# Counting the SBUF way that VectorE and GpSimd share, and TensorE's rates, in a kernel's own list scheduler

## The chip, the cores and the metric

The kernel runs on one core of a Trainium2 chip. The metric is the device time of one launch in microseconds. The engines are named as in the profile: PE is TensorE (PEld its weight loads), DVE is VectorE, ACT is ScalarE, POOL is GpSimd, SP is SyncE, whose queue here only starts DMAs. SBUF is the on-chip memory that all engines read, PSUM the banks into which PE writes.

## The reference, cut to what matters

Two layers of a decoder trunk over 512 tokens of width 1024, all in float32. Each layer has one input projection, three kinds of attention side by side (native sparse attention with compressed, selected and window parts; stick-breaking; forgetting attention), an output projection, a cross attention over 256 memory tokens, and a gated MLP with a causal convolution of three taps.

```python
for i in range(DEPTH):                                   # 2
    h = rms_norm(x, norm_mix[i])
    (q_n, kc, vc, ks_, vs_, kw, vw, g_n,
     q_s, k_s, v_s, q_f, k_f, v_f, f_l) = split_columns(h @ w_in[i])
    ...
    o = jnp.concatenate([o_nsa, o_sb, o_fox], axis=2).reshape(B, S, MIX_WIDTH).astype(x.dtype)
    x = x + o @ w_out[i]
    m = rms_norm(mem, norm_mem[i])
    x = x + memory_cross_attention(rms_norm(x, norm_cross[i]), m,
                                   w_mq[i], w_mk[i], w_mv[i], w_mo[i])
    x = x + conv_gated_mlp(rms_norm(x, norm_ffn[i]), w_up[i], conv_w[i], conv_b[i], w_down[i])
return rms_norm(x, norm_final)

def conv_gated_mlp(h, w_up, conv_w, conv_b, w_down):
    u = h @ w_up                                         # 1024 -> 5632
    u = lax.conv_general_dilated(u, ...) + conv_b        # 3 taps over the tokens
    gate, val = u[..., :D_FF], u[..., D_FF:]
    return (jax.nn.silu(gate) * val) @ w_down
```

## The kernel before, in words

**Numbers in two parts.** A float32 operand of a large product is kept as a high part (rounded to the type fp32r) and a low part (what the rounding left), and a product is three matmuls: high by high, high by low, low by high (`proj_k`). So each weight tile that a DMA brings (`wr`, a "raw" buffer; there are 6) goes through `split`: a cast makes the high part (`w`, ACT or DVE may do it), and a subtraction the low part (also named `w`, DVE or POOL may do it). The pair of `w` tiles is what PE reads; there are 8 such tiles, and the raw buffer is free for the next DMA only after the subtraction.

**Activations.** The residual stream stands in 8 tiles `x` (128 features by 512 tokens). `Norm.tile` makes for each tile the scaled high part `hh` (ACT or DVE), the low part `hl` (DVE alone, a scalar_tensor_tensor), and the square `sq` (ACT), which is added to the running sum `sa` (DVE or POOL). `rstd_bcast` splits `sa` into `ah` and `al`, sums over partitions on PE (`acc`), and ACT makes the reciprocal root `rstd`.

**Stages.** The start loads the `x` tiles and the first weights, and runs the first projections (`pj` tiles in PSUM) together with the norm of the memory tokens (`mem_norm`: tiles `msq`, `mem`, `mh`, `ml`, 16 stores to DRAM named `mk`) and the compression of keys and values (`comp` and `job_comp`: tile `kcx`, whose products start a short chain that ends in the compressed keys `kc`). Then come the attention items of the layer with projections as filler. The cross stage starts with the last part of the output projection (`add_product` with `wout_c`, by halves of the tokens, each tile followed by `nrm2.tile`), goes through the cross attention (`cross_map`), and ends with its output projection (`add_product` with `wmo`, followed by `nrm3.tile`). Then comes the MLP: 22 pairs of up-projections (24 matmuls each), whose results go through `u` and `cv` on DVE and ACT to `gh` and `gl`, and 16 down-projections of 33 matmuls each.

**What sets the order.** All instructions are first recorded as `Op`s, each with its engine (or several that may do it, `alts`), a cost in ns, and dependencies taken from the regions that it reads and writes. `Plan.run` then goes through a planned time: for each engine `pick` takes the first recorded instruction that is ready and whose buffers can be had; `better` passes it over where another allowed engine would end it earlier by the planner's clocks; and the engine with the earliest start goes next. What comes out is the order of each engine's instructions, and for instructions with `alts` the engine. The chip then runs every engine's list strictly in that order, with semaphores between engines. The planner's costs are no times of the chip: they only decide order and place. `Engine.__getattr__` gives each matmul its cost, `_cost` gives the others theirs: of a tensor_tensor over 512 elements 1225 ns on POOL, and 595 on DVE plus the penalty `PEN` of 245 ns that `better` adds for DVE.

The lines of before that the change touches are these:

```python
end = max(t, op.ready[e]) + op.alts[e][1] + self.PEN[e]        # better
...
c = max(64, n) / 2.4                                           # matmul of n columns
if args[1].buf.dtype == FT:
    part = args[1].p1 - args[1].p0 <= 64 or out.p1 - out.p0 <= 64
    c = max(c * (2 if part else 4), 107 if part else 214)
...
return self.plan.add("PE", name, outs, ins, fn, max(c, 104) + 3)
```

In the profile nearly every instruction has the line of the helper that calls it in the end (L385), so groups are told apart by the names of their tiles.

Of the kernel before, what the change touches and what calls it, by code (L numbers as in the profile page):

```python
# [140 lines left out]
class Op:  # L141
    __slots__ = ("i", "eng", "fn", "cost", "tail", "deps", "after", "wait", "ready", "new", "bufs", "prio", "end", "name", "alts")


class Plan:


# [26 lines left out]
    def add(self, eng, name, outs, ins, fn, cost, tail=0, alts=()):  # L174
        op = Op()
        op.alts = {eng: (fn, cost)}
        op.alts.update(alts)
        op.i, op.eng, op.fn, op.cost, op.tail, op.name = len(self.ops), eng, fn, cost, tail, name
        op.prio = op.i + self.bias
        op.deps, op.after, op.new, op.bufs, op.end = {}, [], [], [], None  # L180
        for views, wr in ((ins, False), (outs, True)):
            for v in views:
                b = v.buf
# [23 lines left out]
    def run(self):  # L207
# [16 lines left out]
        for op in self.ops:  # L224
            if not op.wait:
                for e in op.alts:
                    heapq.heappush(soon[e], (0.0, op.prio, op.i))
        dma = 0.0
        order = []
# [33 lines left out]
        def better(e, op, t):  # L263

            if len(op.alts) == 1:
                return False
            end = max(t, op.ready[e]) + op.alts[e][1] + self.PEN[e]
            for x, (_, c) in op.alts.items():
                if x != e and max(clock[x], op.ready[x]) + c + self.PEN[x] < end:
                    c += sum(ops[i].alts[x][1] for p, i in avail[x] if p < op.prio and not done[i])  # L270
                    if max(clock[x], op.ready[x]) + c + self.PEN[x] < end:
                        return True
            return False

        def pick(e):
            t = clock[e]
            while soon[e] and soon[e][0][0] <= t:
                r, p, i = heapq.heappop(soon[e])
                if not done[i]:
                    heapq.heappush(avail[e], (p, i))  # L280
            tried, got, no = [], None, set()
            while avail[e]:
                x = heapq.heappop(avail[e])
                if done[x[1]]:
                    continue
                tried.append(x)
                op = ops[x[1]]
                kinds = {b.kind for b in op.bufs if not b.held}
                if kinds & no:
                    continue  # L290
                if room(op):
                    if better(e, op, t):
                        continue
                    got = op
                    break
                no |= kinds
            for x in tried:
                heapq.heappush(avail[e], x)
            if got is not None:
                return max([t, got.ready[e]] + [min(free[b.kind]) for b in got.bufs if b.kind is not None and not b.held]), got  # L300
            for r, p, i in sorted(soon[e]):
                if not done[i] and room(ops[i]) and not better(e, ops[i], t):
                    return max([t, r] + [min(free[b.kind]) for b in ops[i].bufs if b.kind is not None and not b.held]), ops[i]
            return None

        cand = {e: None for e in self.engines}
        while len(order) < len(ops):
# [10 lines left out]
            for b in made[op.i]:  # L318
# [5 lines left out]
                live[k].append(b)  # L324
            clock[e] = start + op.cost
            op.end = start + op.cost
            if op.tail:
# [25 lines left out]
class Engine:  # L353
# [17 lines left out]
    def __getattr__(self, name):  # L371
        def call(out, *args, **kw):
# [26 lines left out]
            if name == "matmul":  # L399
                n = args[1].size()  # L400
                c = max(64, n) / 2.4
                if args[1].buf.dtype == FT:
                    part = args[1].p1 - args[1].p0 <= 64 or out.p1 - out.p0 <= 64
                    c = max(c * (2 if part else 4), 107 if part else 214)
                if not kw.get("start"):
                    ins = ins + [out]
                return self.plan.add("PE", name, outs, ins, fn, max(c, 104) + 3)
            if name == "transpose":
# [1312 lines left out]
```

## Time and profile before

| | us |
|---|---|
| median of 3 timed runs | 1514.27 |
| lowest and highest of them | 1512.98, 1520.28 |
| the profiled execution, its own time | 1519.45 |
| its span from first to last instruction | 1517.7 |
| PE busy, of that span | 1450.1 |
| DVE, ACT, POOL busy | 1109.1, 669.4, 402.0 |

Busy time is the share in which at least one instruction of an engine is under way. PE's matmuls overlap (a matmul of 512 columns is shown with some 390 ns, but the next starts after 233), so a busy PE is not a PE at its peak. An instruction of DVE or POOL that has started and cannot go on is shown as busy, with a longer duration. The clock granted to TensorE is given as a share of full speed; it is 0.5 or 1 at any moment. A row of the timeline may stand for several instructions of one form (x2, x3): its time is then from the first start to the last end, and the time in square brackets is the idle time before it, with what ended it.

### The profile page before, as it was taken

How to read it: one execution, taken by the hardware profiler on the slowest of the kernel's cores; microseconds unless marked ns; L12 is line 12 of the kernel's file. 1: busy time of each engine (PE TensorE's matmuls, PEld its weight loads, DVE VectorE, ACT ScalarE, POOL GpSimd, SP SyncE). 2: the span in 40 equal slices, each digit the busy share in tenths (PEclk: the TensorE clock that was granted, in tenths of full speed). 3: DMA queues.
4: the chain of work that ended last, by engine and by line, in shares of the span. 5: the costliest groups of instructions: out<-in, count | busy, mean ns of one | idle time of the engine just before them, and what ended most of it. 6: DMA issues, size and time to landing. Idle time of an engine off the chain costs nothing.

```text
span 1517.7 us, 21473 instructions
## 1 busy us (share of the span) xinstructions
PE 1450.1 (96%) x7478; PEld 1156.8 (76%) x7478; DVE 1109.1 (73%) x2166; ACT 669.4 (44%) x1490; POOL 402.0 (26%) x337
## 2 busy tenths in 40 slices
PE   7899999988899999999999999999789999999997
PEld 5777677777888788888887766877778887888886
DVE  7876857789978835887575686677989785378864
ACT  5356566747533213223333656674574322123321
POOL 5321112352422212221143111124542221122111
PEclk9899999999999999999999999999999999999998
DMA  8620214034123233322433121412312223323232
GB/s 260 220 77 29 63 43 129 32 105 132 56 98 97 70 104 105 97 95 83 157 116 99 38 63 49 125 47 83 109 44 91 82 82 92 111 91 97 76 100 69
DMA packets 88556, 140.99 MB, mean 93 GB/s; under 512 B 13088, under 2 KB 35904, under 8 KB 88448
## 3 DMA queue, kind: packets, MB, share of 16 engines
q1 hardware_dynamic: 85696, 136.65, 28.9%
q0 software_dynamic: 1120, 1.41, 0.4%
q10 hardware_dynamic: 1632, 1.57, 0.3%
q8 instruction: 58, 0.95, 0.3%
q14 instruction: 50, 0.41, 0.1%
HBM read 125.04 MB, written 8.39 MB: 88 GB/s over the span
## 4 chain that ended last, share of the span: by engine, by line
PE 72%; DVE 20%; issue 3%; ACT 3%; DMA 2%; SPq 0%; DVEq 0%; ACTq 0%
PE pj L385 39%; PE S L385 25%; DVE w L385 4%; PE acc L385 4%; PE T L385 3%; DVE cv L385 3%; DVE hl L385 2%; DVE x L385 2%; ACT cv L385 1%; DMA wr<-in_dram 1%; DVE u L385 1%; DVE sa L385 1%; DVE sp L385 1%; ACT cp L385 0%; SPq L385 0%
## 5 line engine op out<-in xcount | busy, mean ns | idle before, releaser
L385 POOL TENSOR_TENSOR w<-wr,w 128x512 fp32r<-128x512 f32 (+4 forms) x212 | 299.7, 1420 | 817.1 <-PE pj L385 378.9
L385 PE MATMUL pj<-hh,w 128*128 128x512 f32 (+1 forms) x1376 | 436.7, 389 | 11.6 <-ACT hh L385 7.9
L385 PEld LDWEIGHTS pj<-hh,w 128*128 128x128 f32 x1376 | 256.6, 192 | 68.5 <-ACT hh L385 9.0
L385 ACT ACTIVATE w<-wr 128x512 fp32r<-128x512 f32 (+4 forms) x288 | 160.9, 584 | 284.5 <-PE pj L385 175.7
L385 DVE TENSOR_TENSOR w<-wr,w 128x512 fp32r<-128x512 f32 (+4 forms) x256 | 207.9, 826 | 103.4 <-PE S L385 45.1
L385 PE MATMUL pj<-hl,w 128*128 128x512 f32 (+1 forms) x688 | 265.6, 386 | 2.4 <-DVE hl L385 2.3
L385 PE MATMUL S<-hh,w 128*128 128x512 f32 (+1 forms) x736 | 230.1, 385 | 0.0
L385 DVE SCALAR_TENSOR_TENSOR cv<-u,conv,cv 128x510 f32<-128x510 f32 (+1 forms) x176 | 153.2, 873 | 69.2 <-ACT cv L385 66.0
L385 PEld LDWEIGHTS S<-hh,w 128*128 128x128 f32 x736 | 136.8, 188 | 29.9
L385 PEld LDWEIGHTS pj<-hl,w 128*128 128x128 f32 x688 | 132.0, 192 | 29.8 <-DVE hl L385 5.8
L385 DVE CAST w<-wr 128x512 fp32r<-128x512 f32 (+4 forms) x180 | 77.0, 443 | 94.5 <-PE pj L385 40.4
L385 ACT ACTIVATE cv<-u,conv 128x512 f32<-128x512 f32 x88 | 71.5, 815 | 163.1 <-DVE u L385 163.1
L385 PE MATMUL S<-hl,w 128*128 128x512 f32 (+1 forms) x368 | 141.6, 385 | 0.0
L385 PE MATMUL pj<-oh,w 128*128 128x512 f32 (+1 forms) x320 | 102.6, 373 | 13.8 <-DVE x L385 13.2
L385 PE MATMUL S<-gh,w 128*128 128x512 f32 (+1 forms) x396 | 114.8, 369 | 0.0
L385 PE MATMUL pj<-gh,w 128*128 128x512 f32 x352 | 113.4, 395 | 0.2
L385 ACT ACTIVATE P<-P,nmx 128x512 f32<-128x512 f32 (+3 forms) x160 | 87.9, 552 | 28.9 <-DVE nmx L385 28.6
L385 DVE CUSTOM_DVE_ANT_0 P<-S,maskq 128x512 f32<-128x512 f32 (+3 forms) x160 | 70.4, 486 | 31.7 <-PE S L385 29.7
L385 PEld LDWEIGHTS pj<-oh,w 128*128 128x128 f32 x320 | 60.2, 190 | 28.6 <-DVE x L385 15.4
L385 PEld LDWEIGHTS S<-gh,w 128*128 128x128 f32 x396 | 71.6, 188 | 13.6
L385 PE MATMUL pj<-w,hh 128*128 128x280 f32 (+2 forms) x384 | 80.9, 305 | 0.0
L385 PEld LDWEIGHTS S<-hl,w 128*128 128x128 f32 x368 | 69.2, 188 | 14.9
(266 smaller groups left out, 2460.8 us busy)
## 6 DMA issues: line engine op xcount, KB each, us to landing
wr<-in_dram SPq DMA_DIRECT2D x292, 256.0 KB
wr<-in_dram SPq DMA_DIRECT2D x112, 192.0 KB
wr<-in_dram SPq DMA_DIRECT2D x48, 128.0 KB
x<-in_dram SPq DMA_DIRECT2D x16, 256.0 KB
wr<-in_dram SPq DMA_DIRECT2D x8, 280.0 KB
wr<-in_dram SPq DMA_DIRECT2D x8, 260.0 KB
cw<-in_dram SPq DMA_DIRECT2D x8, 256.0 KB
mk<-mh SPq DMA_DIRECT2D x8, 256.0 KB
```

The lines of the kernel that those rows point to most:

```text
L385: return getattr(eng, name)(real(out), *[real(a) for a in args], **{k: real(v) for k, v in kw.items()})
```

## The change

Two things change in the planner, and nothing in what is computed. First, each `Op` gets a flag `port`, set when none of its tiles is in PSUM and it is no DMA. The planner keeps one time `port` for VectorE and GpSimd together: an instruction with the flag, on either of the two, can't start in the plan before the last one with the flag has ended, on either of the two. `better` counts that wait when it compares engines, and `pick` prefers an instruction that need not wait for it. Second, a matmul's cost is 0.455 ns for each column (at least 110 ns), so that 512 columns cost 233 ns where 216.3 stood; the float32 forms follow 0.835 ns a column, twice that where rows and columns are all in use.

```diff
@@ Plan.add
+        op.port = not tail and not any(v.buf.bank for v in list(ins) + list(outs))
@@ Plan.run
-        dma = 0.0
+        dma = port = 0.0
@@ better
-            end = max(t, op.ready[e]) + op.alts[e][1] + self.PEN[e]
+            end = max(t, op.ready[e], held(op, e)) + op.alts[e][1] + self.PEN[e]
             for x, (_, c) in op.alts.items():
-                if x != e and max(clock[x], op.ready[x]) + c + self.PEN[x] < end:
+                if x != e and max(clock[x], op.ready[x], held(op, x)) + c + self.PEN[x] < end:
                     c += sum(ops[i].alts[x][1] for p, i in avail[x] if p < op.prio and not done[i])
-                    if max(clock[x], op.ready[x]) + c + self.PEN[x] < end:
+                    if max(clock[x], op.ready[x], held(op, x)) + c + self.PEN[x] < end:
                         return True
             return False
+        def held(op, e):
+            return port if op.port and e in ("DVE", "POOL") else 0.0
@@ pick
                     if better(e, op, t):
                         continue
+                    if held(op, e) > t:
+                        later = later or op
+                        continue
                     got = op
                     break
...
+            got = got or later
             if got is not None:
-                return max([t, got.ready[e]] + [...]), got
+                return max([t, held(got, e), got.ready[e]] + [...]), got
@@ Plan.run, after an instruction is placed
             clock[e] = start + op.cost
+            if op.port and e in ("DVE", "POOL"):
+                port = clock[e]
@@ Engine, matmul
-                c = max(64, n) / 2.4
+                c = max(0.455 * n, 110)
                 if args[1].buf.dtype == FT:
                     part = args[1].p1 - args[1].p0 <= 64 or out.p1 - out.p0 <= 64
-                    c = max(c * (2 if part else 4), 107 if part else 214)
+                    c = max(0.835 * n, 107) * (1 if part else 2)
...
-                return self.plan.add("PE", name, outs, ins, fn, max(c, 104) + 3)
+                return self.plan.add("PE", name, outs, ins, fn, c)
```

Both programs hold the same instructions; order and place differ. POOL's list goes from 342 instructions with operands to 226, DVE's from 2168 to 2182, ACT's from 1306 to 1413. The largest moves by kind: of the subtractions for `w` of 512 columns 149 stood on POOL and 93 do now; of the casts for `w` of 512 columns 109 stood on DVE and 38 do now (the others are on ACT); of the additions to `sa` by halves 35 stood on POOL and 8 do now.

In the rows that follow, a name is the program's tile with its number, an underscore and a running number of the build, and the last column is the shape written.

The start of POOL's list, before, behind its constants: `w18` to `w24` are the low parts of the first weights, `sa66` is the sum of squares, `w147` and `w163` the low parts of the next weights, `mem` the memory tokens.

```order
L385 TENSOR_TENSOR w18_148<-wr29_130,w17_144 128x256
L385 TENSOR_TENSOR sa66_146<-sa66_146,sq67_166 128x512
L385 TENSOR_TENSOR w20_196<-wr38_142,w19_185 128x256
L385 TENSOR_TENSOR w20_196<-wr43_162,w19_185 128x256
L385 TENSOR_TENSOR sa66_146<-sa66_146,sq69_211 128x512
L385 TENSOR_TENSOR w22_246<-wr48_182,w21_234 128x256
L385 TENSOR_TENSOR w22_246<-wr53_206,w21_234 128x256
L385 TENSOR_TENSOR sa66_146<-sa66_146,sq71_260 128x512
L385 TENSOR_TENSOR w24_293<-wr58_230,w23_282 128x256
L385 TENSOR_TENSOR w24_293<-wr63_258,w23_282 128x256
```

The same place of POOL's list in the changed program:

```order
L399 TENSOR_TENSOR msq94_402<-msq94_402,msq98_424 128x512
L399 TENSOR_TENSOR w147_456<-wr148_365,w146_437 128x560
L399 DMA rot15_77<-u87_447 8x512 x2
L399 DMA rot16_78<-u125_454 8x512 x2
L399 DMA kcx89_574<-in_18_dram 128x8x2
L399 TENSOR_TENSOR t1124_460<-t1124_460,rot16_78 128x512
L399 TENSOR_TENSOR t1134_515<-t1134_515,rot15_77 128x512
```

All of the first weights' low parts and sums of squares have moved to DVE, and POOL's first instruction with operands is one of the memory norm.

PE's list at the reciprocal root of the memory tokens, before: `acc101` sums the squares over partitions and waits for DVE's `ah` and `al`; `pj133` is the second projection, `pj154` the first tile of a third one of 280 columns.

```order
L385 MATMUL pj133_419<-hh61_299,w23_282 128x512
L385 MATMUL acc101_483<-ah102_469,ones12_74 128x256
L385 MATMUL pj133_419<-hl62_313,w23_282 128x512
L385 MATMUL acc101_483<-al103_480,ones12_74 128x256
L385 MATMUL acc101_483<-ah104_476,ones12_74 128x256
L385 MATMUL pj133_419<-hh61_299,w24_293 128x512
L385 MATMUL acc101_483<-al105_485,ones12_74 128x256
L385 MATMUL pj154_497<-w146_455,hh26_140 128x280
```

And in the changed program:

```order
L399 MATMUL pj158_489<-w146_437,hh26_140 128x280
L399 MATMUL pj158_489<-w147_456,hh26_140 128x280
L399 MATMUL pj154_474<-w147_456,hh36_177 128x280
L399 MATMUL acc101_497<-ah102_487,ones12_74 128x256
L399 MATMUL pj154_474<-w146_437,hl37_187 128x280
L399 MATMUL pj154_474<-w146_437,hh41_203 128x280
L399 MATMUL pj154_474<-w147_456,hh41_203 128x280
L399 MATMUL acc101_497<-al103_495,ones12_74 128x256
L399 MATMUL acc101_497<-ah104_491,ones12_74 128x256
```

`acc101` stands behind all of `pj133` and in the midst of `pj154` now. The first product of `kcx` (`pj126`) has moved behind 13 more matmuls of 280 columns; the second (`pj136`) stands at nearly the same place, and the same 264 matmuls stand ahead of the first `S` in both lists. On SP the loads of the weight for `pj187` (`wr185`, `wr186`) stood ahead of the 16 stores `mk`, and stand behind 15 of them now; on DVE one subtraction for `w151`, the low part that the second half of `pj154` reads, stood ahead of `kcx` and stands behind all of `ml` now.

DVE's list at the beginning of the cross stage, before: `x` takes a product tile (`pj` or `S`, both in PSUM), `hh` and `hl` are its two parts.

```order
L385 TENSOR_TENSOR x727_797<-x727_797,pj878_3505 128x256
L385 TENSOR_SCALAR hh875_3536<-x699_453,gains3_65 128x256
L385 SCALAR_TENSOR_TENSOR hl872_3543<-x688_432,gains3_65,hh871_3524 128x256
L385 SCALAR_TENSOR_TENSOR hl876_3552<-x699_453,gains3_65,hh875_3536 128x256
L385 TENSOR_TENSOR x752_804<-x752_804,S882_3511 128x256
L385 SCALAR_TENSOR_TENSOR hl880_3566<-x727_797,gains3_65,hh879_3549 128x256
L385 TENSOR_TENSOR x760_2357<-x760_2357,pj886_3516 128x256
L385 TENSOR_TENSOR x785_2361<-x785_2361,S890_3521 128x256
L385 SCALAR_TENSOR_TENSOR hl884_3585<-x752_804,gains3_65,hh883_3572 128x256
```

And in the changed program, from the same row:

```order
L399 TENSOR_TENSOR x727_596<-x727_596,pj878_3502 128x256
L399 TENSOR_SCALAR hh875_3528<-x699_426,gains3_65 128x256
L399 SCALAR_TENSOR_TENSOR hl872_3535<-x688_408,gains3_65,hh871_3516 128x256
L399 SCALAR_TENSOR_TENSOR hl876_3543<-x699_426,gains3_65,hh875_3528 128x256
L399 TENSOR_TENSOR sa873_3525<-sa873_3525,sq877_3533 128x256
L399 SCALAR_TENSOR_TENSOR hl880_3557<-x727_596,gains3_65,hh879_3541 128x256
L399 TENSOR_TENSOR sa873_3525<-sa873_3525,sq881_3549 128x256
L399 TENSOR_TENSOR x752_751<-x752_751,S882_3508 128x256
```

The additions to `sa`, which POOL did beside these rows, stand among them on DVE. Over one cross stage (from the first `x` to the last `hl` of `nrm3`) 15 additions to `sa` and 6 subtractions for `w` of 512 columns go from POOL to DVE, 2 and 3 of them the other way; 13 rows go from DVE to ACT (five of `hh`, three casts for `w`, and others) and 7 from ACT to DVE; DVE's list there has 167 rows where 157 stood. The two layers' cross stages change alike. In the MLP, PE's list is the same row for row; in the attention stages a few matmuls at a time change places, most of the groups standing as before.

More of the change, by code (lines that the diff above doesn't have):

```diff
@@ L141 @@
 class Op:
-    __slots__ = ("i", "eng", "fn", "cost", "tail", "deps", "after", "wait", "ready", "new", "bufs", "prio", "end", "name", "alts")
+    __slots__ = ("i", "eng", "fn", "cost", "tail", "deps", "after", "wait", "ready", "new", "bufs", "prio", "end", "name", "alts", "port")
 class Plan:
@@ L280, in pick @@
                     heapq.heappush(avail[e], (p, i))
-            tried, got, no = [], None, set()
+            tried, got, no, later = [], None, set(), None
             while avail[e]:
@@ L298, in pick @@
                 heapq.heappush(avail[e], x)
+            got = got or later
             if got is not None:
-                return max([t, got.ready[e]] + [min(free[b.kind]) for b in got.bufs if b.kind is not None and not b.held]), got
+                return max([t, held(got, e), got.ready[e]] + [min(free[b.kind]) for b in got.bufs if b.kind is not None and not b.held]), got
             for r, p, i in sorted(soon[e]):
                 if not done[i] and room(ops[i]) and not better(e, ops[i], t):
-                    return max([t, r] + [min(free[b.kind]) for b in ops[i].bufs if b.kind is not None and not b.held]), ops[i]
+                    return max([t, r, held(ops[i], e)] + [min(free[b.kind]) for b in ops[i].bufs if b.kind is not None and not b.held]), ops[i]
             return None
```

## The prediction

> **What bounds the kernel now.** I read the page's busy shares, then the busy time by stage, and then, where PE isn't full, DVE's and POOL's rows side by side. The rows below are the page's first part and the windows view; each window row has, after the stretch, its length, busy us (instructions) of PE, PEld, DVE, ACT and POOL, PE's granted clock, DMA share and GB/s.
>
> ```profile
> PE 1450.1 (96%) x7478; PEld 1156.8 (76%) x7478; DVE 1109.1 (73%) x2166; ACT 669.4 (44%) x1490; POOL 402.0 (26%) x337
> ```
>
> ```profile
> 5.00:80.00 75.00, 64.43 (x286) 51.55 (x286) 62.43 (x109) 34.20 (x76) 31.93 (x30) 0.91 0.74 237
> 80.00:324.00 244.00, 237.89 (x1369) 174.03 (x1367) 172.38 (x452) 147.93 (x371) 55.86 (x47) 1.00 0.23 69
> 324.00:405.00 81.00, 67.39 (x493) 62.16 (x494) 77.52 (x160) 54.22 (x145) 35.10 (x35) 0.94 0.31 96
> 405.00:788.00 383.00, 382.16 (x1698) 310.88 (x1698) 271.43 (x412) 115.94 (x190) 91.58 (x66) 1.00 0.32 101
> 788.00:1063.00 275.00, 268.39 (x1546) 200.38 (x1544) 187.41 (x474) 157.07 (x394) 66.74 (x58) 1.00 0.25 73
> 1063.00:1145.00 82.00, 68.16 (x490) 63.48 (x491) 77.36 (x160) 54.22 (x145) 35.14 (x35) 0.92 0.24 75
> 1145.00:1500.00 355.00, 354.09 (x1546) 287.40 (x1545) 249.83 (x380) 101.51 (x162) 79.24 (x56) 1.00 0.28 88
> ```
>
> PE's 96% is a mean over unlike stages: the start, then attention, cross stage and MLP of layer 1, and the same three of layer 2. In the MLPs (383 and 355 us, half the span) PE is busy to within 1 us at full clock. In the cross stages (81 and 82 us) it is DVE that is full, 77.5 and 77.4 us, with POOL busy 35 us beside it, while PE's clock falls to 0.94 and 0.92. The chain of waits, cut to the first cross stage, agrees: nearly all of it is DVE's.
>
> ```profile
> by line: DVE hl L385 21.9%; DVE x L385 12.2%; DVE w L385 8.1%; DVE sa L385 7.3%; issue 6.3%; PE pj L385 6.1%; DVE nmx L385 5.5%; DVE cpl L385 4.2%; DVE hh L385 4.2%; DVE stb L385 3.8%; PE acc L385 2.3%; DVE dhl L385 2.0%; DVE os L385 2.0%;
> ```
>
> Whether DVE and POOL get in each other's way there is read from the timeline of the stage's second half, where POOL runs six subtractions in a row (POOL's row, then DVE's):
>
> ```profile
> 389.38 8.56 POOL L385 TENSOR_TENSOR w<-wr,w 128x512 fp32r<-128x512 f32 x6 [0.93 <-PE S L385]
> ```
>
> ```profile
> 389.72 1.53 DVE L385 SCALAR_TENSOR_TENSOR hl<-x,gains,hh 128x256 fp32r<-128x256 f32 x1
> 391.17 1.48 DVE L385 TENSOR_TENSOR sa<-sa,sq 128x256 f32<-128x256 f32 x1
> 392.57 0.41 DVE L385 TENSOR_TENSOR x<-x,pj 128x256 f32<-128x256 f32 x1
> ...
> 393.86 2.94 DVE L385 SCALAR_TENSOR_TENSOR hl<-x,gains,hh 128x256 fp32r<-128x256 f32 x2
> 396.73 1.50 DVE L385 TENSOR_TENSOR sa<-sa,sq 128x256 f32<-128x256 f32 x1
> ...
> 401.60 0.47 DVE L385 SCALAR_TENSOR_TENSOR hl<-x,gains,hh 128x256 fp32r<-128x256 f32 x1
> 402.00 0.41 DVE L385 TENSOR_TENSOR sa<-sa,sq 128x256 f32<-128x256 f32 x1
> ```
>
> With POOL idle (the last two rows) `hl` takes 0.47 and `sa` 0.41; beside POOL both take about 1.5. `x`, one operand of which is in PSUM, keeps its 0.41 in the midst of it. So a DVE row that touches only SBUF waits out a POOL instruction, and others don't: what the planner now counts exists.
>
> **The change, part by part: the cross stages.** *One `sa` moved.* In the first half of the stage POOL does five `sa` beside DVE's `hl` and `hh`. Busy time in that stretch of DVE's `hl` (with a stretch after POOL is done for comparison), of POOL's `sa`, and the least, middle and longest duration of `hh` in ns:
>
> ```profile
> 325.80:331.60 5.80, 4.29 (x6) 0.77 0.21 72
> 399.00:402.40 3.40, 1.42 (x3) 1.00 0.31 88
> ```
>
> ```profile
> 325.80:331.60 5.80, 0.00 (x0) 0.00 (x0) 0.00 (x0) 0.01 (x1) 3.71 (x5) 0.77 0.21 72
> L385 DVE TENSOR_SCALAR hh<-x,gains x2: 337/574/810, 329.5 to 332.5; 128x256 fp32r<-128x256 f32 x2
> ```
>
> Six `hl` took 4.29 where six free ones take 2 × 1.42 = 2.84; one `hh` took 0.81 where the free one takes 0.34. That is 1.45 + 0.47 = 1.92 us for five `sa`, 0.38 each. On DVE the addition costs about 0.34 (0.41, less the 0.07 by which rows here overlap: 401.60 to 402.00 is 0.40 for a row of 0.47). A move gains 0.04, and 15 less 2 of them 0.5 us.
>
> *One `w` moved.* The six `w` stretched 1.53, 1.48, 2.94 and 1.50 from 0.47, 0.41, 0.87 and 0.41: 5.3 us, 0.88 each. On DVE one costs 0.67 when POOL is idle:
>
> ```profile
> 66.81 0.67 DVE L385 TENSOR_TENSOR w<-wr,w 128x512 fp32r<-128x512 f32 x1
> ```
>
> Gain 0.21; for 6 less 3 that is 0.6 us. *Rows that ACT takes:* 13 go and 7 come; six fewer at 0.34 or more (`hh`) make 2.0 us, and ACT, busy 54 of 81 us, has the room. Together 3.1 us a stage, and as DVE sets the pace here it is time: **6 us** in both. Bounds: were no wait to go, DVE would have 13 × 0.34 + 3 × 0.67 − 2.0 = 4.4 more in each; had every moved instruction held DVE as long as a `w` does, 13 × 0.54 + 0.6 + 2.0 = 9.6 less. I take the value of the rows, which are of this stage itself.
>
> **The start.** PE waits here, and its clock falls behind the waits (two windows, then PE's timeline):
>
> ```profile
> 25.00:50.00 25.00, 22.27 (x116) 18.83 (x115) 21.86 (x35) 9.84 (x19) 11.84 (x13) 0.93 0.69 221
> 50.00:80.00 30.00, 26.01 (x127) 22.46 (x126) 22.45 (x49) 12.02 (x33) 7.59 (x7) 0.83 0.72 237
> ```
>
> ```profile
> 39.70 0.39 PE L385 MATMUL acc<-ah,ones 128*128 128x256 f32 x1 [1.52 <-DVE ah L385]
> 39.93 0.39 PE L385 MATMUL pj<-hl,w 128*128 128x512 f32 x1
> 41.34 0.38 PE L385 MATMUL acc<-al,ones 128*128 128x256 f32 x1 [1.03 <-DVE al L385]
> ...
> 54.87 2.82 PE L385 MATMUL pj<-kcx,cw 128*128 128x66 f32 x16 [2.06 <-DVE kcx L385]
> ...
> 80.32 1.98 PE L385 MATMUL S<-kc,t 64*128 64x32 f32 x32
> ```
>
> Three waits make 4.6 us; the clock costs 0.07 × 25 + 0.17 × 30 = 6.9, as PE work at half speed. So at least 11.5 us lie ahead of the first `S` at 80.32, with the same 264 matmuls ahead of it in both lists. The new order puts filler ahead of the `acc` waits and takes POOL's first dozen subtractions and sums off it. Against that stands a new wait: one subtraction for `w151` is behind all of `ml` on DVE, and 44 matmuls of 280 columns and 38 of 512 are behind it on PE. PE's steady rate (24 matmuls of 512 columns, a piece of the chain) and the last of `ml`:
>
> ```profile
> 582.01 5.60 PE pj L385 x24
> ```
>
> ```profile
> 54.84 4.05 DVE L385 SCALAR_TENSOR_TENSOR ml<-mem,gains,mh 128x256 fp32r<-128x256 f32 x10
> ```
>
> At 0.233 for 512 columns and 0.128 for 280 those matmuls are 14.5 us. DVE ends `ml` at 58.9 now. Its list up to there holds about as much work as before; I allow 2.5 us because POOL has four additions and subtractions there where seven stood. Then 56.4, 0.9 for the rows between, 14.5, and 3.5 for another stretch at half clock and short waits: 75.3, **5 us** earlier. Bounds: 0 (the wait for `w151` eats it all) and −10 (most of the 11.5). On SP, `wr185` and `wr186` now queue behind 15 `mk` stores that wait for `ml`; they are needed only behind the first `S`, some 15 us later. The DMA that starts the second `kcx` moves to POOL's queue behind two `rot` DMAs; POOL has little else there.
>
> By the Trainium skill, "TensorE: Matmul & The Clock Gate", section "Part 1: The HAM clock gate (the "warmup" mystery)", the clock halves after an idle window of about 3.4 us. No wait quoted here is that long, and yet the rows have 0.83, so the row decides. By the page's figure alone, closing these gaps would bring no clock back, and this term would be about 2 us.
>
> **Attention.** PE is busy 237.9 of 244 and 268.4 of 275 us, DVE some 70%, PE's order nearly the same. DVE's waits behind POOL reach PE seldom: **1 us** a layer, bounds −4 and +4, since in such chains one row at another place gains or costs a wait of 1 to 2 us.
>
> **The MLPs:** 0. PE's list is the same, and the new rate changes only the plan. DVE has 271 of 383 us; the subtractions that come to it are set off by casts that go to ACT (116 of 383). Were that cover gone, PE would wait for weights: up to +4 for both. **The end:** 0, bounds ±1; the last `y` rows go from POOL to DVE.
>
> **Sum:** 5 + 6 + 2 = 13 us off the profiled execution's 1519.45 is 1506.5. That execution lies 5.2 above the timed median; the four times known (1512.98, 1514.27, 1519.45, 1520.28) have their middle at 1516.9, and 13 less is **1504**.
>
> **Rivals.** *ACT or a chain takes DVE's place.* For it: ACT gets 107 more instructions, in order ahead of `hh` and the exponentials, and cross attention is a chain PE, DVE, ACT, PE, which needs no engine to be full. Against: ACT is busy 54 of 81 us. If half of the 13 rows that come to ACT in a cross stage delay an `hh` by 0.5, the 3 us are gone in both; start and attention leave about 5: 1512.
>
> *DVE carries more than it is freed from* (slower). POOL did part of its `sa` while DVE worked from PSUM, at no cost; moved, each costs 0.34. It decides at 0.34 of wait per `sa` removed, and I measured 0.38 over five. At 0.1, and with `w` likewise near 0.3, it is 4 us in each cross stage; in the start, where DVE gets 15 more rows at about 0.5, up to 7: 1532.
>
> *Full clock comes back* (faster still). The clock costs 6.9 in the start and 0.06 × 81 + 0.08 × 82 = 11.4 in the cross stages. If PE's gaps become too short to drop it, some 15 us come on top of the forecast: 1489. For it: the gaps follow DVE's locked rows. Against: DVE still sets the pace.
>
> **How the numbers follow.** Forecast 0.46 (1495 to 1507), full clock 0.16 (1489), ACT or chains 0.26 (1512), DVE overloaded 0.12 (1532). A measurement of this kernel can tell about 0.5%, 7.6 us, from no change. Faster takes the forecast and the full clock, 0.62; same 0.26; slower 0.12. The range leaves out most of the slower case and the tail of the faster one: 1484 to 1520.
>
> **What would show it.** Right: POOL's busy time falls by a third; `hl` of 256 columns and `w` of 512 on DVE come near 0.47 and 0.67; the cross stages take 78 to 79 us; the first `S` comes near 75; both MLPs keep their length. Wrong: a first `S` at 80 or later with PE waiting for `w`; cross stages of 81 us with DVE still full; PE idle in an MLP; ACT as the releaser of the longest waits.

## The result and the profile after

The changed kernel takes 1480.91 us (median of 4 runs, 1479.96 to 1483.36), before takes 1514.81 in the same comparison: a ratio of 0.977, 95% interval 0.975 to 0.978. That is 34 us where 13 were forecast, and 3 us below the low end of the range. The profiled execution took 1483.36, with a span of 1481.6 us, 36.1 shorter than that of before.

The first part of the page and the windows view of the changed kernel (after the stretch: length, then busy us of PE, PEld, DVE, ACT and POOL, PE's granted clock, DMA share, GB/s). The edges are the same matmuls as those near the prediction's edges.

```profile
PE 1433.5 (97%) x7478; PEld 1156.4 (78%) x7478; DVE 1015.1 (69%) x2180; ACT 725.5 (49%) x1595; POOL 263.5 (18%) x221
```

```profile
5.00:79.20 74.20, 61.49 (x287) 49.90 (x288) 56.26 (x122) 34.97 (x79) 16.92 (x14) 0.88 0.72 239
79.20:317.90 238.70, 237.30 (x1369) 175.43 (x1369) 164.40 (x447) 157.41 (x388) 44.01 (x40) 1.00 0.23 70
317.90:390.70 72.80, 63.85 (x488) 61.34 (x487) 68.88 (x166) 55.30 (x151) 20.62 (x18) 0.95 0.31 99
390.70:771.60 380.90, 380.90 (x1704) 311.79 (x1703) 243.80 (x406) 134.78 (x223) 58.12 (x41) 1.00 0.32 103
771.60:1039.30 267.70, 266.03 (x1546) 200.93 (x1545) 180.43 (x481) 163.32 (x404) 48.89 (x46) 1.00 0.25 74
1039.30:1112.30 73.00, 63.69 (x489) 61.37 (x488) 68.81 (x166) 55.64 (x151) 20.87 (x19) 0.95 0.25 77
1112.30:1464.60 352.30, 352.30 (x1549) 288.40 (x1548) 222.74 (x369) 119.69 (x194) 50.49 (x35) 1.00 0.28 91
```

| us gained, profile against profile | measured | forecast |
|---|---|---|
| start, to the first `S` (80.3, now 79.2) | 1.1 | 5 |
| attention of layers 1 and 2 | 5.7, 8.4 | 1, 1 |
| cross stages | 7.4, 8.3 | 3, 3 |
| MLPs | 2.2, 2.3 | 0 |
| end | 0.7 | 0 |

POOL's busy time fell by a third, as forecast. PE runs the same 7478 matmuls. Its idle time fell from 67.6 to 48.1 us, everywhere but in the start, and its busy time by 16.6; a matmul behind a wait or at half clock is shown longer, but how much of the 16.6 that makes isn't shown. The groups of DVE in the first cross stage, by form (before, then after, then `hl` of *cross_places*, an experiment below that has the engines of the changed kernel in the order of before; the numbers behind the bar are busy us and the mean ns of one):

```profile
L385 DVE SCALAR_TENSOR_TENSOR hl<-x,gains,hh 128x256 fp32r<-128x256 f32 x32 | 23.5, 750 | 0.2
...
L385 DVE TENSOR_TENSOR w<-wr,w 128x512 fp32r<-128x512 f32 x5 | 6.5, 1337 | 0.0
```

```profile
L399 DVE SCALAR_TENSOR_TENSOR hl<-x,gains,hh 128x256 fp32r<-128x256 f32 x32 | 17.3, 554 | 0.6 <-ACT hh L399 0.6
...
L399 DVE TENSOR_TENSOR w<-wr,w 128x512 fp32r<-128x512 f32 x7 | 4.6, 687 | 0.1
```

```profile
L423 DVE SCALAR_TENSOR_TENSOR hl<-x,gains,hh 128x256 fp32r<-128x256 f32 x32 | 17.3, 545 | 0.6 <-ACT hh L423 0.4
```

```profile
L399 DVE SCALAR_TENSOR_TENSOR hl<-x,gains,hh x32: 465/474/1521, 318.6 to 389.5; 128x256 fp32r<-128x256 f32 x32
```

The same 32 `hl` take 6.2 us less (the middle one of them 0.474 us, as the view by tile has it in ns, least, middle and longest), though POOL still has 17 additions and subtractions in the stage. In *cross_places* they take as little, so the places are enough for that, without the new order. What the new order does with rows that stay on POOL shows in the timeline of the stage's second half (DVE's rows with their start and duration, then POOL's):

```profile
379.10 0.42 DVE L399 TENSOR_TENSOR sa<-sa,sq 128x256 f32<-128x256 f32 x1
379.44 0.41 DVE L399 TENSOR_TENSOR x<-x,S 128x256 f32<-128x256 f32 x1
379.77 0.41 DVE L399 TENSOR_TENSOR x<-x,pj 128x256 f32<-128x256 f32 x1
...
382.75 0.41 DVE L399 TENSOR_TENSOR x<-x,S 128x256 f32<-128x256 f32 x1
383.08 2.54 DVE L399 SCALAR_TENSOR_TENSOR hl<-x,gains,hh 128x256 fp32r<-128x256 f32 x5
```

```profile
380.23 1.30 POOL L399 TENSOR_TENSOR w<-wr,w 128x512 fp32r<-128x512 f32 x1 [3.48 <-DVE x L399]
381.47 2.68 POOL L399 TENSOR_TENSOR sa<-sa,sq 128x256 f32<-128x256 f32 x3
```

Eleven `x` rows, which read PSUM, now stand in a row at their free 0.41 us, beside most of POOL's four rows. In the timeline of before in the prediction, `hl` and `sa` stand there and wait 1 us each.

### The profile page after: what moved, and what is told of

Same layout as the page of the kernel before. It is cut to its first block, busy times and chain, and to the rows that moved or that the text cites. A ratio compares the mean times of both kernels' runs of the same rounds, so it can differ in the third digit from the quotient of the medians.

```text
span 1481.6 us, 21384 instructions
## 1 busy us (share of the span) xinstructions
PE 1433.5 (97%) x7478; PEld 1156.4 (78%) x7478; DVE 1015.1 (69%) x2180; ACT 725.5 (49%) x1595; POOL 263.5 (18%) x221
## 4 chain that ended last, share of the span: by engine, by line
PE 83%; DVE 6%; ACT 3%; issue 1%; DMA 1%; POOL 0%; DVEq 0%; POOLq 0%; ACTq 0%
PE pj L399 44%; PE S L399 31%; PE acc L399 4%; PE T L399 3%; DVE sp L399 2%; ACT cp L399 1%; DMA wr<-in_dram 1%; DVE x L399 1%; DVE w L399 1%; ACT sp L399 0%; DVE sa L399 0%; DVE sb L399 0%; DVE hl L399 0%; ACT w L399 0%; DVE y L399 0%
## 5 line engine op out<-in xcount | busy, mean ns | idle before, releaser
L399 PE MATMUL pj<-hh,w 128*128 128x512 f32 (+1 forms) x1376 | 429.7, 384 | 5.5 <-ACT hh L399 5.5
L399 ACT ACTIVATE w<-wr 128x512 fp32r<-128x512 f32 (+4 forms) x363 | 201.8, 590 | 364.7 <-PE pj L399 229.0
L399 POOL TENSOR_TENSOR w<-wr,w 128x512 fp32r<-128x512 f32 (+4 forms) x142 | 207.0, 1462 | 966.2 <-PE S L399 376.1
L399 DVE TENSOR_TENSOR w<-wr,w 128x512 fp32r<-128x512 f32 (+3 forms) x326 | 207.7, 660 | 177.7 <-PE pj L399 76.2
L399 PEld LDWEIGHTS pj<-hh,w 128*128 128x128 f32 x1376 | 253.2, 189 | 60.5 <-ACT hh L399 6.2
L399 PE MATMUL pj<-hl,w 128*128 128x512 f32 (+1 forms) x688 | 261.8, 381 | 0.4 <-DVE hl L399 0.4
L399 DVE SCALAR_TENSOR_TENSOR cv<-u,conv,cv 128x510 f32<-128x510 f32 (+1 forms) x176 | 131.4, 749 | 72.6 <-ACT cv L399 69.7
L399 ACT ACTIVATE cv<-u,conv 128x512 f32<-128x512 f32 x88 | 71.6, 815 | 62.5 <-DVE u L399 62.4
L399 DVE CAST w<-wr 128x512 fp32r<-128x512 f32 (+4 forms) x105 | 39.5, 402 | 82.2 <-issue 53.6
L399 PEld LDWEIGHTS pj<-gh,w 128*128 128x128 f32 x352 | 66.3, 188 | 14.8
```

The lines of the kernel that those rows point to most:

```text
L399: return getattr(eng, name)(real(out), *[real(a) for a in args], **{k: real(v) for k, v in kw.items()})
```

## The experiments

The first four tell the two halves of the change apart, and places from order. In *port_only* TensorE's old rates are back, in *rates_only* `held` returns 0:

```diff
-                c = max(0.455 * n, 110)
+                c = max(64, n) / 2.4
...
-            return port if op.port and e in ("DVE", "POOL") else 0.0
+            return 0.0
```

> The shared way is counted, TensorE's old rates stay. Three theories for the 34 us that the change gained. Lock theory (the planner keeps SBUF rows of DVE and POOL apart, and that alone removes the waits): within 5 us of the changed kernel, 1478 to 1486, cross stages near 73 us where they were 81. Rates theory (true TensorE rates let the plan put DVE's work where PE really waits for it): at most a third of the gain, 1503 or more. Both-needed theory: near half, 1493 to 1500. In the start the lists differ from the changed kernel's: both subtractions for w151 stand on DVE ahead of the second kcx, so whichever theory holds I expect the first S some 3 us ahead of the changed kernel's 79.2.

> TensorE's new rates alone, the shared way isn't counted; POOL has 321 rows where before had 342. Lock theory: no change within 4 us of before, 1511 to 1519, cross stages still 80 us. Rates theory: most of the gain, 1480 to 1492. Both-needed theory: 1500 to 1508.

In *place_only* the plan is made twice, and only the engines of the first go into the second; *order_only* has True and False exchanged (`count` switches `held`):

```diff
+        self.count = True
+        self.place()
+        for op in self.ops:
+            op.alts = {op.eng: op.alts[op.eng]}
...
+        self.count = False
+        order, made = self.place()
```

> The plan is made twice with the new rates: once counting the shared way, from which only the engine of each instruction is kept, and once more not counting it, which sets the order. So the places are those of the changed kernel, the order is blind to the shared way. Theory P (what counts is that POOL has a third fewer rows, whenever they run): 1478 to 1488. Theory O (what counts is that the remaining rows run at times when the other engine works from PSUM): 1500 or more. If both share it: 1488 to 1500.

> The reverse: places as the plan with the new rates gives them without counting the shared way (POOL 321 rows), the order counts it. Theory P: no gain to speak of, 1508 to 1518. Theory O: 1480 to 1492, with DVE's rows in the cross stage free of waits although POOL does as much as before. If both share it: 1493 to 1505.

Measured, with all that follows. A ratio is to the runs of before beside it, with its 95% interval; the stages are those of one profile each. Attention of layer 2 is counted here from the end of the layer's first projections.

| | median | ratio | first `S` | attention 1 | cross 1 | attention 2 | cross 2 |
|---|---|---|---|---|---|---|---|
| before | 1514.8 | | 80.3 | 244.4 | 80.3 | 235.0 | 81.3 |
| before_again | 1519.6 | one run | 80.7 | 244.2 | 80.3 | 234.8 | 81.1 |
| the change | 1480.9 | 0.975 to 0.978 | 79.2 | 238.7 | 72.9 | 225.3 | 73.0 |
| after_again | 1480.9 | one run | 79.4 | 238.7 | 71.6 | 225.3 | 71.8 |
| port_only | 1479.4 | 0.973 to 0.977 | 66.1 | 244.6 | 77.6 | 226.0 | 77.5 |
| rates_only | 1538.4 | 1.012 to 1.016 | 76.3 | 249.5 | 86.7 | 235.6 | 83.7 |
| place_only | 1498.1 | 0.986 to 0.990 | 75.6 | 241.0 | 76.8 | 229.5 | 76.9 |
| order_only | 1503.0 | 0.989 to 0.992 | 79.7 | 239.6 | 80.0 | 227.1 | 78.9 |
| old_pen1200 | 1500.0 | 0.988 to 0.991 | 74.1 | 238.1 | 83.1 | 228.0 | 82.5 |
| cross_places | 1511.3 | 0.996 to 0.998 | 76.6 | 244.2 | 79.2 | 235.1 | 79.2 |
| cross_back | 1494.3 | 0.983 to 0.986 | 78.2 | 238.7 | 78.7 | 225.3 | 77.9 |
| att_places | 1525.2 | 1.003 to 1.007 | 78.9 | 243.2 | 82.0 | 235.1 | 82.7 |
| att_back | 1490.8 | 0.981 to 0.984 | 78.4 | 241.9 | 72.2 | 230.9 | 72.9 |
| nopool | 1494.7 | 0.983 to 0.987 | 79.3 | 235.3 | 81.0 | 223.0 | 81.0 |
| early151 | 1478.3 | 0.974 to 0.976 | 74.9 | 238.7 | 72.3 | 225.3 | 72.2 |
| w151_dve | 1480.4 | 0.975 to 0.977 | 75.6 | 238.7 | 73.1 | 225.3 | 72.7 |
| late554 | 1470.6 | 0.969 to 0.971 | 63.1 | 242.9 | 72.4 | 225.4 | 72.9 |
| late_nopool | 1473.9 | 0.967 to 0.972 | 64.4 | 237.2 | 78.8 | 222.3 | 79.2 |

Attention of layer 2 gains 9.7 here and 8.4 in the table above, which counts it from an earlier matmul.

The lock theory holds in its total: the shared way alone gives all of the gain. It misses twice: TensorE's rates alone don't leave the time as it is, they make the kernel 1.4% slower, and port_only reaches the time of the change by another road, with a start 13 us shorter (3 were expected) and cross stages 4.7 longer. With the new rates, places alone gain 40 us on rates_only and order alone 35, and both together 57: each does much, and they overlap (the expectation that both share it, in both runs).

Nearly all that port_only lacks in a cross stage is one wait, 4.5 us in both (DVE's rows, PE's, then DVE's again):

```profile
333.62 0.76 DVE L399 TENSOR_TENSOR al<-sa,ah 128x256 fp32r<-128x256 f32 x2
```

```profile
338.25 0.28 PE L399 MATMUL acc<-ah,ones 128*128 128x256 f32 x1
```

```profile
339.45 0.70 DVE L399 TENSOR_TENSOR w<-wr,w 128x512 fp32r<-128x512 f32 x1 [4.47 <-ACT rstd L399]
```

`al` is ready at 334.4, but PE, busy without a gap, reaches `acc` only at 338.3, behind projections that stand ahead of it in its list, and DVE stands idle for 4.47, by the profile until `rstd` is there.

*old_pen1200* asks whether any plan with less on POOL does as well: `PEN` of POOL is 1200 in before, and nothing else is changed.

```diff
-    PEN = {"ACT": 0, "DVE": 245, "POOL": 0, "SP": 0}
+    PEN = {"ACT": 0, "DVE": 245, "POOL": 1200, "SP": 0}
```

> Before, with POOL made dearer by 1200 ns in the planner's comparison of engines and nothing else: POOL has 223 rows besides DMAs where port_only has 199 and before some 320, the order is blind to the shared way. If less load on POOL is all that counts: 1480 to 1490. If the time at which the remaining rows run counts as much: 1495 to 1508. If the load that goes to DVE instead of ACT costs as much as the waits: 1510 or more.

It gains 1.1%, as much as the middle theory said. Attention is nearly as short as in the change; the cross stages, where DVE has 184 rows for 157, are longer than before. So less on POOL helps where DVE has room, and hurts where it has none.

**The cross stages, row for row.** *cross_places* takes the prediction's term by itself: the list of before in its order, and after planning, in the two cross stages, the engine that the changed plan (`keep`) chose. *cross_back* is the reverse.

```diff
         for pos, op in enumerate(order):
+            e = keep[op.i]
+            if op.eng != e and not op.tail and any(a <= pos < z for a, z in spans):
+                op.eng, (op.fn, op.cost) = e, op.alts[e]
```

> The order of before, row for row, but in the two cross stages each instruction that has a choice of engines runs on the engine that the changed kernel gave it (15 sums and 6 subtractions from POOL to DVE, and the other moves of that stage). This is the term of the prediction by itself. Theory A (the prediction's price of the moved rows was right, 3.1 us a stage; the other 4 to 5 us a stage that were measured come from the order, in which the rows that stay on POOL no longer meet SBUF rows of DVE): 1508 to 1512 where before has 1515, cross stages 76 to 78 us. Theory B (the moved rows alone bring the whole 7.4 and 8.3): 1498 to 1502, cross stages 73. Theory C (DVE overloaded): 1515 or more.

> The kernel before, profiled once more, because cross_places had its first S at 76.6 where the profile of before has 80.3, though both have the same lists up to there. If the start is the part that differs from execution to execution: first S anywhere from 76 to 81, attention of layer 2 and the cross stages within 1 us of the first profile (235.0, 80.3, 81.3). If the cross stages themselves vary by 2 us, no gain of cross_places in them is shown.

> The changed kernel, profiled once more: first S at 79 within 2 us, cross stages 73 within 0.5, attention of layer 2 225 within 1. It sets what early151's first S of 74.9 is worth.

> The reverse of cross_places: the order of the changed kernel, row for row, but in the two cross stages each instruction that has a choice runs on the engine that before gave it (POOL has 35 additions and subtractions there, not 17). Theory A (order and places each bring half of the cross stages' gain): cross stages 76 to 78, total 1488 to 1492. Theory D (neither helps without the other, since an order that was made for other places makes engines wait for each other): cross stages 79 or more, total 1494 or more. Theory E (the order alone brings it): cross stages 73 to 75, total 1481 to 1485.

The repeats set the scale: the cross stages of before vary by 0.2 us, those of the change by 1.3 (0.5 was expected), and the first `S` of programs with the start of before came from 76.6 to 80.7, with that of the change from 78.2 to 79.4. The moved places alone gain 1.1 and 2.1 us, the order alone 1.6 and 3.4, both 7.4 and 8.3. So theory D comes nearest: most of the gain needs both. The match isn't clean: cross_places has the total of theory A (1511.3) without its stages, and the second cross stage of cross_back (77.9) lies in theory A's range. The windows view, for before between the same matmuls and then for cross_places, shows where the gain stays, and the waits view of DVE (us in total, times, longest) what for:

```profile
324.70:404.90 80.20, 67.28 (x492) 62.04 (x493) 76.72 (x158) 54.22 (x145) 35.00 (x35) 0.94 0.31 95
320.90:400.10 79.20, 66.78 (x492) 61.57 (x493) 71.54 (x173) 56.45 (x150) 17.81 (x15) 0.96 0.30 95
```

```profile
DVE cpl L423 <- ACT cph L423: 2.1, 2, 1.5
DVE os L423 <- ACT ot L423: 1.1, 2, 0.7
```

DVE's busy time falls by 5.2 us, but its idle time grows from 3.5 to 7.7: above all it waits for ACT, longer than before (0.5 and 0.7 in these two rows there), in an order that was made for other places. That is the prediction's first rival, in this version of the kernel. In the changed kernel DVE has 166 rows between these matmuls where cross_places has 173, and is busy 68.9 us and idle 3.9.

**What POOL is still worth.** In *nopool* POOL gets no instruction that another engine may do.

```diff
-    PEN = {"ACT": 0, "DVE": 245, "POOL": 0, "SP": 0}
+    PEN = {"ACT": 0, "DVE": 245, "POOL": 100000, "SP": 0}
```

> The changed kernel with POOL closed to every instruction that has a choice: no wait at the shared way at all, and some 180 more rows on DVE. If what remains on POOL in the changed kernel costs more than it helps: 1481 or less, attention of layer 2 under 225. If POOL still helps where DVE is full: attention 224 to 227, cross stages 77 to 80 (9 subtractions of 0.67 and 6 sums of 0.41 more on DVE, less 6 us of waits), total 1486 to 1496.

```profile
314.60:395.50 80.90, 66.40 (x481) 62.16 (x481) 73.82 (x191) 51.28 (x140) 0.00 (x0) 0.94 0.27 81
818.90:1041.80 222.90, 222.53 (x1290) 165.57 (x1289) 156.38 (x447) 154.58 (x388) 0.00 (x0) 1.00 0.24 71
```

Without any wait at the shared way the cross stage is as long as before. DVE has 191 rows there and is busy 4.9 us longer than in the changed kernel; the other 3.2 are idle time of DVE, with 2.4 in one wait for ACT's `hh`. In attention of layer 2 the kernel is 2.3 us faster, and PE waits only 0.4 us in 223. Beside the changed kernel, in these plans, POOL is worth 8 us in each cross stage and costs 3.4 and 2.3 in the attention stages. The total is that of the second theory, with cross stages 1 us longer than it said; attention, with 223.0, is that of the first.

**Attention, row for row.** *att_places* and *att_back* are cross_places and cross_back with the spans from each layer's first `S` to its cross stage.

> The order of before, row for row, but between the first S of each layer and its cross stage each instruction that has a choice runs on the engine that the changed kernel gave it. Attention of layer 2 took 235.0 before, 225.3 in the changed kernel, 223.0 with POOL closed. If the places bring it, since PE's waits there hang on single rows of DVE that a POOL row held up: 226 to 229, total 1500 to 1505. If the order does: 233 to 235, total 1511 to 1516. If, as in the cross stages, neither helps alone: 231 to 234.

> The reverse: the order of the changed kernel, in the two attention stages the engines of before. If the places bring the gain: attention of layer 2 at 231 to 235, total 1491 to 1497. If the order does: 225 to 227, total 1481 to 1485. If neither alone: 229 to 234, as far back as att_places is.

Places alone bring nothing in attention of layer 2 (235.1 for 235.0), order alone 4.1 of 9.7; in layer 1 they bring 1.2 and 2.5 of 5.7. So in layer 2, as in the cross stages, most of the gain needs both: att_back lies in the range of its third theory, att_places gained even less than its third theory said. PE waits for DVE's `x` there 2.2 us where it waited 3.0, but also for ACT, which it didn't in that stage of before:

```profile
PE T L423 <- ACT P L423: 1.8, 2, 1.4
```

The total of att_places is slower than before by 0.5%; the profile is of its fastest execution (1518.33, the other six 1523 to 1528), so where the others lose their 7 us isn't shown.

**The start.** Three versions: *early151* puts the two subtractions for `w151` first in the planner's queue, *w151_dve* moves one instruction after planning, *late554* counts the old rates for what is recorded ahead of the first `S` (instruction 554).

```diff
-        op.prio = op.i + self.bias
+        op.prio = op.i + self.bias - 1000 * (eng in ('DVE', 'POOL') and outs[0].buf.name == 'w151')
```

```diff
+            if op.eng == "POOL" and not op.tail and op.bufs[-1].name == "w151":
+                op.eng, (op.fn, op.cost) = "DVE", op.alts["DVE"]
```

```diff
+                old = len(self.plan.ops) < 554
+                if old:
+                    c = max(64, n) / 2.4
...
```

> The changed kernel with the two subtractions for w151 put first in the planner's queue: they stand on DVE ahead of the memory norm's split and of both kcx, and behind the first S the lists are those of the changed kernel. If the late w151 is what kept the start from gaining: first S at 68 to 72 us where it was 79.2, total 1470 to 1474. If the start is bound by the chain of kcx or by transfers: first S at 77 or later, total 1478 to 1482.

> The changed kernel, every list row for row, but one instruction: the second subtraction for w151, which ran on POOL for 4.49 us (56.85 to 61.34) while DVE's SBUF rows stood back to back until 60.1, is on DVE, next to the first. If this row is what the start's term missed (0.9 us allowed from the last ml to a full w151, 5.4 measured): PE's wait of 2.66 us goes, first S at 75.5 to 76.7 where it was 79.2 and 79.4, total 1477 to 1478.5. If PE only waits elsewhere instead (its clock is at half there, or the next w is late): first S at 78 or later, total 1480 to 1482.

> TensorE's old rates for the instructions recorded ahead of the first S, the new ones behind it, the shared way counted throughout: the start of port_only joined to the rest of the changed kernel. If the two parts are independent: first S at 66 to 67, cross stages 73, total 1466 to 1472, faster than both kernels. If what the start gains is given back (weights and the stored memory tokens come no earlier): attention of layer 1 longer by 5 or more, total 1476 or more.

What w151_dve takes away is this (the changed kernel: PE's rows of the start with their waits in brackets, then DVE's and POOL's rows):

```profile
51.93 3.68 PE L399 MATMUL pj<-kcx,cw 128*128 128x66 f32 x16 [4.93 <-DVE kcx L399]
56.97 0.60 PE L399 MATMUL pj<-w,hh 128*128 128x280 f32 x1 [1.35 <-DVE w L399]
...
61.40 0.60 PE L399 MATMUL pj<-w,hh 128*128 128x280 f32 x1 [2.66 <-POOL w L399]
```

```profile
51.91 4.05 DVE L399 SCALAR_TENSOR_TENSOR ml<-mem,gains,mh 128x256 fp32r<-128x256 f32 x10
...
57.00 0.68 DVE L399 TENSOR_TENSOR w<-wr,w 128x512 fp32r<-128x512 f32 x1
...
57.70 0.68 DVE L399 TENSOR_TENSOR w<-wr,w 128x512 fp32r<-128x512 f32 x1
```

```profile
32.58 1.85 POOL L399 TENSOR_TENSOR w<-wr,w 128x560 fp32r<-128x560 f32 x1
...
56.85 4.49 POOL L399 TENSOR_TENSOR w<-wr,w 128x560 fp32r<-128x560 f32 x1
```

Here POOL is the one that waits: DVE's rows keep their free 0.68 one behind the other, and POOL's subtraction, of a size that took 1.85 us earlier in the same start, ends 4.49 after it began. In w151_dve that wait of PE is gone, and the first `S` comes at 75.6:

```profile
57.04 0.60 PE L401 MATMUL pj<-w,hh 128*128 128x280 f32 x1 [2.02 <-DVE w L401]
```

The start is 3.6 us shorter in the profile, and the stages behind it are unchanged, but the timed ratio can't be told from that of the change, and the median (1480.4) missed its range by 2 us; whether the whole 3.6 reaches the end is open. early151 comes to 74.9 and 1478.3, between its two theories: a late `w151` was one cause among several. late554 joins port_only's start to the change's cross stages, as its first theory said, and is the fastest that was run, 3.0% under before. Attention of layer 1 gives back 4.2 of the 16.1 us by which its start is shorter than that of the change. PE's waits in its start are short (63.1 is its first `S`):

```profile
47.95 2.00 PE L399 MATMUL pj<-kcx,cw 128*128 128x66 f32 x16 [0.59 <-DVE kcx L399]
58.37 0.72 PE L399 MATMUL pj<-hh,w 128*128 128x512 f32 x2 [1.08 <-DVE w L399]
```

*late_nopool* is late554 and takes POOL from everything with a choice that is recorded between a layer's first `S` and its cross stage:

```diff
+            if len(op.alts) > 1 and not op.tail and any(at[a] <= op.i < at[z] for a, z in (("S176", "S898"), ("S1727", "S2449"))):
+                op.alts.pop("POOL", None)
```

> late554 with POOL closed to everything with a choice that is recorded from the first S of each layer to its cross stage. From nopool (attention of layer 2 at 223.0 for 225.4, attention of layer 1 some 3 us shorter) 1464 to 1467 against late554's 1470.6, if cross stages stay at 73. If the new plan moves rows in the cross stages too and these come to 76: 1470 to 1474.

Both attention stages get shorter, by 5.7 (behind a start 1.3 longer) and 3.1, but the new plan has cross stages of 79 us, with one wait of 3.9 for `rstd` like that of port_only. Its second theory holds, and it isn't faster than late554 (one of its five runs was 1464.72, the others 1471 to 1475).

## Why the forecast fell short, step by step

- **What bounds the kernel: right.** DVE in the cross stages, waits in the start, PE in the MLPs; and the shared way is real. The chain of the first cross stage was read too strongly: its row gives DVE 71%, not nearly all. As forecast, `w` of 512 columns on DVE came to 0.69 us, and `hl` to a median near its free 0.47.
- **The cross stages: right in kind, the size less than half.** The step that failed is the price of the moved rows ("A move gains 0.04", and 0.21 for a `w`). With what ACT takes over, it made 3.1 us of DVE's time a stage; between the same matmuls of the first one DVE's busy time fell by 7.8, from 76.7 to 68.9, and that became 7.4 us of time. Read from five `sa` and six `w`, the price was too low for the stage as a whole. Summed over all DVE rows of the stage, what they take beyond the middle duration of the same form in nopool, where POOL has nothing beside them, is some 17 us in before and 6 in the changed kernel; the prediction's prices take 13 × 0.38 + 3 × 0.88 = 7.6 off. The places do that alone (6 in cross_places; the order alone leaves 14), and DVE's busy time fell by 5.2 with them. But there the stages got only 1.1 and 2.1 us shorter, as DVE waited for ACT instead. So "as DVE sets the pace here it is time" needs the new order as well, for which the forecast had no term, though the diff changes the order too (`pick` passes over a row that must wait). What it is in the new order that avoids those waits wasn't tried. Its bound of 9.6 a stage did hold.
- **Attention: the step that failed most**, 2 forecast and 14 measured. "DVE's waits behind POOL reach PE seldom" was argued from shares of busy time. The waits view of before, from 788 to 1064.1 us, would have shown what there was to gain:

```profile
PE pj L385 <- DVE x L385: 3.0, 2, 1.7
PE T L385 <- DVE cs L385: 1.6, 2, 0.9
PE S L385 <- DVE x L385: 1.2, 1, 1.2
PE T L385 <- DVE P L385: 1.0, 1, 1.0
PE S L385 <- DVE nmx L385: 0.8, 1, 0.8
```

That is 7.6 us in seven waits; the changed kernel has 1.5 in all there, and with POOL closed (nopool) 0.4 were left. So 6.1 of the 8.4 us gained are waits of PE; the rest is busy time of PE, for which no cause is shown. A wait like the longest, in layer 1, with what DVE and POOL did ahead of it:

```profile
266.65 1.23 DVE L385 TENSOR_TENSOR sb<-sb,sb 128x256 fp32r<-128x256 f32 x1
267.80 1.76 DVE L385 TENSOR_TENSOR w<-wr,w 128x512 fp32r<-128x512 f32 x1
...
270.42 0.67 DVE L385 TENSOR_TENSOR x<-x,pj 128x512 f32<-128x512 f32 x1
```

```profile
266.29 1.30 POOL L385 TENSOR_TENSOR sp<-sp,sp 128x384 fp32r<-128x384 f32 x1 [0.72 <-ACT sb L385]
267.56 1.45 POOL L385 TENSOR_TENSOR w<-wr,w 128x512 fp32r<-128x512 f32 x1
```

```profile
271.15 0.50 PE L385 MATMUL pj<-oh,w 128*128 128x512 f32 x1 [1.69 <-DVE x L385]
```

`w` lost 1.1 us (0.67 when free) behind POOL's two rows, and `sb` more than half of its 1.23 (rows of that size take 0.41); `x` came that much later, and PE waited 1.69. That moving such rows away isn't enough shows in att_places. By the Trainium skill, "SBUF — State Buffer", section "SBUF: two separate sides", a VectorE instruction with two SBUF inputs and a GpSimd instruction that reads SBUF shut each other out for the whole instruction, by a lock on ports that they share. The rows agree: `sb` and `w`, both with two inputs in SBUF, took 1.23 and 1.76 beside POOL's.
- **The start: one number of the sum was wrong.** DVE ended `ml` at 56.0 (56.4 forecast), and from a full `w151` to the first `S` it took 17.8 us (14.5 and 3.5 forecast). But from `ml` to the full `w151` it took 5.4, not 0.9: one of the two subtractions for `w151` was on POOL, and POOL's row waited for DVE's. The forecast had let only DVE wait. w151_dve shows it: 75.6, where 75.3 was forecast and where the start of the change has 78.2 to 79.4. The three waits counted there (4.6 us) gave place to longer ones, those of 4.93, 1.35 and 2.66 quoted above. Since the first `S` of before's start varies from 76.6 to 80.7, the 1.1 us measured can't be told from none. And there was more to gain than the 11.5 us counted: late554, another plan, has a start 17 us shorter than that of before.
- **The MLPs: 0 forecast, 2.2 and 2.3 measured.** PE's idle time there, 0.8 and 0.9 us, is gone in the changed kernel; it was above all a wait for DVE's `al`. Where the rest comes from isn't shown.
- **The rivals.** Full clock didn't come back: 0.95 in the cross stages, where 0.94 and 0.92 stood, and 0.88 in the start, where 0.91 stood. The other two turned up only in versions of the kernel: ACT's chain in cross_places and att_places, a DVE with too much in nopool and old_pen1200.

## What to carry to other kernels

Where a planner learns of a shared resource, a price for each moved row, read from a few rows, can be far from that of the stage: sum how much longer than free ones the rows are, over the whole stage. That sum is no forecast of the time either: with the places alone it fell by 11 us in the first cross stage, and the stage by 1.1, since DVE then waited for ACT. And work that leaves the resource has to go somewhere: nopool has none of these waits, and cross stages as long as before. Where PE is nearly full, the list of its few waits is the better estimate (here 7.6 us in attention of layer 2, of which 6.1 went); a share of busy time isn't one. And look at both sides of a lock: a row that is off the path can be kept waiting until it is on it.

## What the runs showed that was not expected

TensorE's true rates made the plan worse by 1.4% without the shared way, and better by 0.5% with it, where they count only for what is recorded behind the first `S` (late554 against port_only, ratios of 0.970 and 0.975). In the start of the changed kernel the granted clock stayed at half from 50 to 63 us, with PE busy 7 of these 13 us, behind the wait of 4.93 quoted above:

```profile
50.00:63.00 13.00, 7.05 (x29) 6.53 (x30) 10.01 (x25) 0.29 (x2) 5.41 (x2) 0.50 0.65 228
```

In late554, whose waits there are near 1 us or less, it was 1.00 from 50 to 63. No wait of several us is needed for that: in the kernel before, the clock fell at 42.2 us, behind waits of 1.52 and 1.03 (the prediction quotes them) that left PE busy 1.46 of 3.42 us:

```profile
38.77:42.19 3.42, 1.46 (x8) 1.10 (x9) 3.42 (x5) 0.00 (x0) 2.04 (x2) 1.00 0.76 236
42.19:45.60 3.41, 3.41 (x17) 3.41 (x16) 3.35 (x6) 1.29 (x3) 2.00 (x2) 0.50 0.38 113
```

And the cross stage of one and the same program took 72.9 in one execution and 71.6 in another.
